# Lower bounds formed later, a first block scaled in halves, transposes on two PSUM tags and unread matmuls, in a stick-breaking and HGRN2 block on one core

## The chip, the core and the metric

The kernel runs on one core of one Trainium2 chip. A core has five engines, each working off its own instruction queue in order: TensorE (PE in the profile, with its weight loads as PEld), VectorE (DVE), ScalarE (ACT), GpSimd (POOL) and SyncE (SP, which here only issues transfers). Engines wait for each other through semaphores. The metric is the device time of one execution in microseconds (us); smaller is better.

## The reference

One residual block works on 16 learned meta rows followed by 1024 frames, each 1024 wide, all in float32:

```python
u = _rmsnorm(h, norm_g[l])
proj = u @ w_in[l]
(sb_q, sb_k, sb_v, sb_gate, hg_q, hg_f, hg_i, hg_gate,
 gate_sb, gate_hg) = jnp.split(proj, bounds, axis=-1)
y_sb = _stick_breaking(sb_q, sb_k, sb_v) * silu(sb_gate)
o_hg = _group_rmsnorm(_hgrn2(hg_q, hg_f, hg_i, lb_all[l]), hg_norm_g[l])
y_hg = o_hg * silu(hg_gate)
merged = (sigmoid(gate_sb) * (y_sb @ w_sb_out[l])
          + sigmoid(gate_hg) * (y_hg @ w_hg_out[l]))
h = h + merged @ w_out[l]
return _rmsnorm(h, final_norm_g)[:, N_META:N_META + S]
```

The lower bounds `lb_all` are a softmax over two rows of logits, one bound for each of 512 key channels. They enter only the forget gate of the HGRN2 branch, `f = lb + (1 - lb) * sigmoid(f_logit)`.

## The kernel before

**Whole program.** A float32 factor is kept as a rounded high part and a low remainder, and a product is three TensorE matmuls (high by high, high by low, low by high). In time order the program has a start (norm, transposes), four first projection groups of 128 columns (`first_g`), the wide projections made with seven products for eight (`prep`, `product`, the matmuls of L410), the attention with further projections laid between, the recurrence, and the output projection. This case is about the first two.

**The start.** The 1040 rows are nine blocks b0 to b8 of 128 rows (b8 has 16). `norm_g` is spread over the partitions into `gbc` by two matmuls with a row of ones (L146) and two VectorE copies (L147). For each block, in this order in the code:

- `stats`: ScalarE squares the block and sums it (L172), GpSimd makes the inverse root (L173, L174) into an `s` tile.
- `scaled`: VectorE multiplies the block `xb` by that and by `gbc`, in place (L180); TensorE transposes it in two halves of four 128 x 128 pieces (L185), each half into a PSUM tile of tag `tr`, which has two buffers; ScalarE rounds each half into `uh` (L187).
- `low_part`: VectorE writes the remainder into `ul` (L195), and ScalarE copies the PSUM half back into `xb` as floats (L196). A `tr` buffer is free once L187, L195 and L196 have read it.

Weights arrive as `wr` and are split in four quarters by ScalarE (`wh`, L119) and VectorE (`wl`, L124), for the first group behind b0 and for the second behind b2; those of the third group (`w3`, L224 and L225) stand behind b3. At the end VectorE forms sums and differences of the blocks for the seven products (`further`, L205 to L213).

**The first groups.** Groups 0, 1 and 2 are taken together by quarters of the rows: 24 matmuls of each group on rows 0 to 255 (blocks b0 and b1), then of each on the next quarter, and so on (`first_q`); group 3 follows alone. An accumulator is one of three PSUM buffers of tag `acc`; ScalarE copies it out (L320), and the copy goes to DRAM from ScalarE's queue.

**What sets the order.** The code above is written once, and a scheduler of the tile framework places each engine's instructions by its own estimates; the engines then run their lists strictly in order. The lower bounds stand late in the code:

```python
V.tensor_tensor(lbd, lbl[:, 0], lbl[:, 1], op=ALU.subtract)
omlb = sb("omlb", [P, 4])
S.activation(lb, lbd, AF.Sigmoid)
S.activation(omlb, lbd, AF.Sigmoid, scale=-1.0)
```

They have no other input than a small transfer (L84), and the scheduler places them at the head of the lists of VectorE and ScalarE. Their first reader is the forget gate (L704), in the attention.

Of the kernel before, what the change touches and what calls it, by code (L numbers as in the profile page):

```python
# [11 lines left out]
AF = mybir.ActivationFunctionType  # L12
ALU = mybir.AluOpType
PSUM = bass.MemoryType.PSUM

P = 128
D = 1024
# [4 lines left out]
NB = SEQ // P  # L22
# [23 lines left out]
def block_kernel(ctx: ExitStack, tc: tile.TileContext, x, meta, norm_g, w_in, w_sb_out,  # L46
                 w_hg_out, w_out, hg_norm_g, hg_lb_logits, final_norm_g, out):
    nc = tc.nc
    V, S, G, T = nc.vector, nc.scalar, nc.gpsimd, nc.tensor
# [5 lines left out]
    def nm(s):  # L55
        uid[0] += 1
        return f"{s}_{uid[0]}"
# [7 lines left out]
    def sb(tag, shape, dt=F32):  # L65
        p = base if tag in HOME else here[-1]
        return p.tile(shape, dt, tag=tag, name=nm(tag), bufs=BUFS.get(tag, 1))

    def ps(tag):
        return psum.tile([P, 512], F32, tag=tag, name=nm(tag), bufs=PB[tag])  # L70

    def kept(name, shape, dt=F32):
        return dram.tile(shape, dt, tag=name, name=nm(name))
# [4 lines left out]
    ident = sb("ident", [P, P])  # L78
    make_identity(nc, ident)
    mhalf = sb("mhalf", [P, 8])  # L80
    G.memset(mhalf, -0.5)

    lbl = sb("lbl", [P, 2, 4])
    nc.gpsimd.dma_start(lbl, hg_lb_logits.rearrange("r (h p) -> p r h", p=P))  # L84
# [12 lines left out]
    def fetch_w(src, col, chunks):  # L97
        if chunks > NC // 2:
            raw = sb("wr", [P, NC, P])
        else:  # L100
            if not half_rows:
                t = sb("wl", [P, 2, NC // 2, P])
                half_rows.extend((t[:, 0], t[:, 1]))
            half_rows.reverse()
            raw = half_rows[0]
        nc.sync.dma_start(raw[:, :chunks], src[:, col:col + P].rearrange("(c p) n -> p c n", p=P))
        return raw
# [20 lines left out]
    uh = sb("uh", [P, NC, L], F32R)  # L128
    ul = sb("ul", [P, NC, L], F32R)
    ones = sb("sg", [1, P])  # L130
# [7 lines left out]
    start = ExitStack()  # L138
    here.append(start.enter_context(phase("start")))

    gbc = sb("gbc", [P, D])
    row = sb("w3", [1, D])
    nc.scalar.dma_start(row, norm_g)
    for hf in range(2):
        acc = ps("acc")
        T.matmul(acc, ones, row[:, hf * 512:(hf + 1) * 512], start=True, stop=True)  # L146
        V.tensor_copy(gbc[:, hf * 512:(hf + 1) * 512], acc)  # L147

    FIRST = [C_HI + P * h for h in range(4)] 
    w3 = sb("w3", [P, 2, NC, P], F32R)  # L150
    xbs, raws = [], []
    for b in range(NB + 1):
# [9 lines left out]
        if b in (1, 3):  # L162
            raws.append(fetch_w(w_in[0], FIRST[b // 2], NC))
    w_first = []

    blk = [dict(rows=P if b < NB else NM, t0=P * b) for b in range(NB + 1)]
# [10 lines left out]
    def scaled(b):  # L177
        v = blk[b]
        rows, xs = v["rows"], xbs[b]
        V.scalar_tensor_tensor(xs[:rows], xs[:rows], v["r"][:rows, 0:1], gbc[:rows], op0=ALU.mult, op1=ALU.mult)  # L180
        v["tp"] = []
        for c4 in range(2):
            tp = ps("tr").rearrange("p (c n) -> p c n", c=4)
            for c in range(4):
                T.transpose(tp[:, c, :rows], xs[:rows, (c4 * 4 + c) * P:(c4 * 4 + c + 1) * P], ident[:rows, :rows])  # L185
            v["tp"].append(tp[:, :, :rows])
            S.activation(uh[:, c4 * 4:c4 * 4 + 4, v["t0"]:v["t0"] + rows], v["tp"][c4], AF.Copy)  # L187

    def low_part(b):

# [24 lines left out]
    for b in range(NB + 1):  # L215
        stats(b)
        scaled(b)
        low_part(b)
        if b in (0, 2):
            w_first.append(load_w(None, None, NC, raws[b // 2], eng=V))  # L220
        if b == 3:
            raw = fetch_w(w_in[0], FIRST[2], NC)
            for c in range(0, NC, SH):
                S.activation(w3[:, 0, c:c + SH], raw[:, c:c + SH], AF.Copy)  # L224
                V.tensor_tensor(w3[:, 1, c:c + SH], raw[:, c:c + SH], w3[:, 0, c:c + SH].bitcast(F32), op=ALU.subtract)  # L225
            w_first.append((w3[:, 0], w3[:, 1]))
# [13 lines left out]
    def proj(col, pieces, evac, begin=None, after=()):  # L240
        return group(w_in[0], col, NC, pieces, u_operand, evac, begin, after)
# [75 lines left out]
    def keep_raw(to):  # L317
        def ev(acc, t0, n):
            c = sb("sg", [P, 512])
            S.activation(c[:, :n], acc, AF.Copy)  # L320
            nc.scalar.dma_start(to[:, t0:t0 + n], c[:, :n])
        return ev

    kept_i = [kept(f"hi{h}", [P, L]) for h in range(4)]
    kept_f = [kept(f"hf{h}", [P, L]) for h in range(len(FIRST) - 4)]
    first_g = [proj(FIRST[h], QUART if h < 3 else FULL, keep_raw((kept_i + kept_f)[h])) for h in range(len(FIRST))]
    for g, w in zip(first_g, w_first):
# [333 lines left out]

    lb = sb("lb", [P, 4])
    lbd = sb("lbd", [P, 4])
    V.tensor_tensor(lbd, lbl[:, 0], lbl[:, 1], op=ALU.subtract)
    omlb = sb("omlb", [P, 4])
    S.activation(lb, lbd, AF.Sigmoid)
    S.activation(omlb, lbd, AF.Sigmoid, scale=-1.0)

    masks, anchor = {}, []

# [576 lines left out]
```

## Time and profile before

| | |
|---|---|
| median of 3 runs | 941.91 us (940.26 to 943.6) |
| profiled execution | 941.53 us |
| its span in the trace | 939.7 us |
| TensorE busy | 900.0 us, 96% of the span |
| VectorE, ScalarE, GpSimd busy | 675.0, 390.6, 248.7 us |

The span is the time between the first and the last recorded instruction; 1.83 us of the execution lie around it. Rows of the timeline give the start in us, the busy time in us, the engine, the line, the operation, what it writes and reads with shapes, the count, and in brackets how long the engine stood idle before it and what ended that. Where several instructions are merged into a row, the busy time is of all of them. The lines on which the prediction rests are quoted there.

### The profile page before, as it was taken

What the parts mean: (1) busy time and instruction counts of PE and PEld (TensorE: products, weight loads), DVE (VectorE), ACT (ScalarE), POOL (GpSimd) and SP (SyncE); (2) the same over time, 40 slices, a digit from 0 to 9 for tenths busy, and PEclk for the clock granted to TensorE, in tenths of its full rate; (3) what the DMA queues carried; (4) which work ended last, traced back from release to release, by engine and by line L of the source; (5) the groups of instructions that cost most, each with busy time, mean ns of one, the idle gap of its engine ahead of it and who ended that gap; (6) DMA issues with size and microseconds to landing.
All of it is one profiled execution on the core that took longest, in us unless ns stands there. A gap on an engine that the chain in (4) does not pass through costs nothing. (4 is left out here: it accounts for less than half of the span.)

```text
span 939.7 us, 13713 instructions
## 1 busy us (share of the span) xinstructions
PE 900.0 (96%) x5000; PEld 781.4 (83%) x5000; DVE 675.0 (72%) x1242; ACT 390.6 (42%) x892; POOL 248.7 (26%) x263
## 2 busy tenths in 40 slices
PE   5999999999999999999999999998989899999996
PEld 4898888888889998898898888897968688888885
DVE  5893446555433477888887898868697788897886
ACT  6824333343333455555565565132314145323341
POOL 3026445544442211132111111121212000003552
PEclk9999999999999999999999999999999999999999
DMA  8123543333336122221132222121111338564212
GB/s 271 52 63 100 160 145 112 101 118 118 113 113 184 63 80 78 68 68 57 57 113 64 72 80 79 57 79 57 56 56 45 102 101 284 186 213 163 107 45 91
DMA packets 89078, 98.04 MB, mean 104 GB/s; under 512 B 4513, under 2 KB 63777, under 8 KB 89010
## 3 DMA queue, kind: packets, MB, share of 16 engines
q1 hardware_dynamic: 75120, 73.51, 25.6%
q10 hardware_dynamic: 13826, 23.64, 6.9%
q8 instruction: 40, 0.66, 0.3%
q14 instruction: 28, 0.23, 0.1%
q0 software_dynamic: 64, 0.01, 0.1%
HBM read 71.94 MB, written 25.20 MB: 103 GB/s over the span
## 5 line engine op out<-in xcount | busy, mean ns | idle before, releaser
L264 PE MATMUL acc<-uh,wh 128*128 128x346 f32 (+4 forms) x536 | 192.3, 359 | 0.0
L264 PE MATMUL acc<-ul,wh 128*128 128x346 f32 (+4 forms) x536 | 184.9, 345 | 0.4 <-DVE ul L195 0.4
L264 PE MATMUL acc<-uh,wl 128*128 128x346 f32 (+4 forms) x536 | 183.9, 343 | 0.0
L124 POOL TENSOR_TENSOR wl<-wr,wh 128x256 fp32r<-128x256 f32 x92 | 80.4, 897 | 361.1 <-ACT wh L119 345.6
L264 PEld LDWEIGHTS acc<-uh,wl 128*128 128x128 f32 x536 | 101.5, 189 | 6.6
L264 PEld LDWEIGHTS acc<-uh,wh 128*128 128x128 f32 x536 | 101.7, 190 | 3.9 <-ACT uh L187 0.2
L264 PEld LDWEIGHTS acc<-ul,wh 128*128 128x128 f32 x536 | 101.9, 190 | 3.4 <-DVE ul L195 0.7
L399 POOL TENSOR_TENSOR pw<-su,pw 128x512 fp32r<-128x512 f32 x44 | 58.5, 1349 | 51.2 <-ACT pw L398 51.2
L572 ACT ACTIVATE ab<-z 128x456 f32<-128x456 f32 (+6 forms) x112 | 50.0, 448 | 30.7 <-PE z L570 30.4
L575 DVE TENSOR_TENSOR_SCAN ab<-ab,later 128x456 f32<-128x456 f32 (+3 forms) x64 | 55.2, 863 | 6.0 <-ACT ab L572 5.4
L615 DVE TENSOR_TENSOR wt<-tr,wt 128x512 fp32r<-128x512 f32 (+1 forms) x80 | 50.3, 630 | 12.6 <-ACT wt L614 11.0
L399 POOL TENSOR_TENSOR pw<-wr,pw 128x512 fp32r<-128x512 f32 x33 | 43.6, 1321 | 54.7 <-ACT pw L398 54.6
L410 PE MATMUL acc<-th,pw 128*128 128x512 f32 x176 | 57.8, 389 | 0.0
L626 PE MATMUL av<-wt,v 128*128 128x256 f32 x320 | 54.1, 287 | 3.6 <-DVE wt L615 2.0
L570 PE MATMUL z<-stk,q 128*128 128x456 f32 (+6 forms) x224 | 56.6, 333 | 0.0
L614 ACT ACTIVATE wt<-tr 128x512 fp32r<-128x512 f32 (+1 forms) x80 | 44.2, 555 | 29.3 <-PE tr L612 29.0
L119 ACT ACTIVATE wh<-wr 128x256 fp32r<-128x256 f32 x100 | 36.3, 410 | 47.5 <-PE acc L264 25.0
L398 ACT ACTIVATE pw<-su 128x512 fp32r<-128x512 f32 x44 | 26.2, 627 | 68.9 <-DVE su L393 47.8
L626 PEld LDWEIGHTS av<-wt,v 128*128 128x128 f32 x320 | 46.8, 188 | 8.6 <-DVE wt L615 4.0
L789 DVE COPY_PREDICATED ab<-mask,z 128x192 f32<-128x192 uint8 (+2 forms) x144 | 45.3, 350 | 11.0 <-PE z L780 9.7
L579 DVE TENSOR_TENSOR_SCAN ab<-ab 128x348 f32<-128x348 f32 (+4 forms) x48 | 46.9, 976 | 6.9 <-ACT ab L572 5.5
L780 PE MATMUL z<-wt,stk 128*128 128x192 f32 x192 | 37.8, 332 | 10.9 <-DVE wt L771 9.8
(335 smaller groups left out, 2057.1 us busy)
## 6 DMA issues: line engine op xcount, KB each, us to landing
wr<-in_w_in SPq DMA_DIRECT2D x48, 512.0 KB, 4.2
q<-q SPq DMA_DIRECT2D x32, 256.0 KB, 4.1
wr<-in_w_out SPq DMA_DIRECT2D x16, 512.0 KB, 4.2
sg<-gate SPq DMA_DIRECT2D x24, 256.0 KB, 3.6
gate<-sg ACTq DMA_DIRECT2D x20, 256.0 KB, 2.0
xb<-in_x SPq DMA_DIRECT2D x7, 512.0 KB, 8.5
gate<-co ACTq DMA_DIRECT2D x12, 256.0 KB, 2.6
pt<-hi SPq DMA_DIRECT2D x4, 520.0 KB, 3.2
```

Source lines behind the costliest of these rows:

```text
L124: eng.tensor_tensor(lo[:, cs], raw[:, cs], h[:, cs].bitcast(F32), op=ALU.subtract)
L264: T.matmul(acc, a, b, start=(k == 0), stop=(k == total - 1))
L399: G.tensor_tensor(t[:, 1], d[key], t[:, 0].bitcast(F32), op=ALU.subtract)
L410: T.matmul(acc, t[:, part // 2, c], (bh, bl, bh)[part][:, c], start=(c == part == 0), stop=(c == 3 and part == 2))
L570: T.matmul(z, qt[:, k, qo + qi * P:qo + (qi + 1) * P], st["k"][hh][:, c0:c1], start=(k == 0), stop=(k == 1))
L572: S.activation(a[:, c0:c1], z, AF.Sigmoid, scale=-1.0)
L575: ins = V.tensor_tensor_scan(w, w, later[:, WS - (n - c0):][:, ::-1], 1.0, op0=ALU.mult, op1=ALU.max)
L579: V.tensor_tensor_scan(w, w, w, a[:, c1:c1 + 1], op0=ALU.mult, op1=ALU.bypass)
L614: S.activation(wt[:, 0, lo:], tp[:, lo:], AF.Copy)
L615: V.tensor_tensor(wt[:, 1, lo:], tp[:, lo:], wt[:, 0, lo:].bitcast(F32), op=ALU.subtract)
L626: T.matmul(self.av, st["v"][hh][:, 2 * gg + j], wt[:, part, where[j]:where[j] + 256], start=(gg == g and part == 0 and j == 0), stop=False)
L789: V.copy_predicated(dst[:, :, :, d * h:], mask[:, :, :, :n * h].to_broadcast([P, 2, m, n * h]), z[:, :, k, :, lo * h:(lo + n) * h])
```

## The change

Four edits, all in the start:

```diff
     G.memset(mhalf, -0.5)
+    S.activation(sb("s4", [P, 8]), mhalf, AF.Square)
...
     for hf in range(2):
         acc = ps("acc")
-        T.matmul(acc, ones, row[:, hf * 512:(hf + 1) * 512], start=True, stop=True)
+        spread = T.matmul(acc, ones, row[:, hf * 512:(hf + 1) * 512], start=True, stop=True)
         V.tensor_copy(gbc[:, hf * 512:(hf + 1) * 512], acc)
 
+    def keep_busy(n, after):
+
+        with tc.issue_after(after.ins):
+            idle = ps("av")
+            for _ in range(n):
+                T.matmul(idle[:, :P], ident, ident, start=True, stop=True)
+
+    keep_busy(10, spread)
...
-        V.scalar_tensor_tensor(xs[:rows], xs[:rows], v["r"][:rows, 0:1], gbc[:rows], op0=ALU.mult, op1=ALU.mult)
+        for cs in ((slice(0, 512), slice(512, D)) if b == 0 else (slice(0, D),)):
+            v["scaled"] = V.scalar_tensor_tensor(xs[:rows, cs], xs[:rows, cs], v["r"][:rows, 0:1], gbc[:rows, cs],
+                                                 op0=ALU.mult, op1=ALU.mult)
         v["tp"] = []
         for c4 in range(2):
-            tp = ps("tr").rearrange("p (c n) -> p c n", c=4)
+            tp = ps(("tr", "z")[b % 2]).rearrange("p (c n) -> p c n", c=4)
             for c in range(4):
-                T.transpose(tp[:, c, :rows], xs[:rows, (c4 * 4 + c) * P:(c4 * 4 + c + 1) * P], ident[:rows, :rows])
+                last = T.transpose(tp[:, c, :rows], xs[:rows, (c4 * 4 + c) * P:(c4 * 4 + c + 1) * P], ident[:rows, :rows])
             v["tp"].append(tp[:, :, :rows])
-            S.activation(uh[:, c4 * 4:c4 * 4 + 4, v["t0"]:v["t0"] + rows], v["tp"][c4], AF.Copy)
+            v["last"] = S.activation(uh[:, c4 * 4:c4 * 4 + 4, v["t0"]:v["t0"] + rows], v["tp"][c4], AF.Copy)
+        if b == 0:
+            keep_busy(8, last)
...
-    V.tensor_tensor(lbd, lbl[:, 0], lbl[:, 1], op=ALU.subtract)
     omlb = sb("omlb", [P, 4])
-    S.activation(lb, lbd, AF.Sigmoid)
-    S.activation(omlb, lbd, AF.Sigmoid, scale=-1.0)
+    with tc.issue_after(blk[NB]["scaled"].ins):
+        V.tensor_tensor(lbd, lbl[:, 0], lbl[:, 1], op=ALU.subtract)
+    with tc.issue_after(blk[NB]["last"].ins):
+        S.activation(lb, lbd, AF.Sigmoid)
+        S.activation(omlb, lbd, AF.Sigmoid, scale=-1.0)
```

The lower bounds are placed behind the last block's scaling and rounding; a Square on eight columns at the head of ScalarE's list loads its table there. Block b0 is scaled in two halves. Odd blocks are transposed into tag `z` (two buffers, not used otherwise this early), even ones into `tr`. Ten matmuls of the identity by itself follow the two that spread `norm_g`, and eight more the transposes of b0; nothing reads what they write. The scheduler then lays out the lists of TensorE, VectorE and ScalarE anew over the start and the first groups; behind the first few weight parts of the seven products each engine's list is as before, and those of GpSimd and SyncE are the same throughout.

TensorE, from the beginning of its list, before (`xb_102`, `xb_105` are blocks b0 and b1, `acc_427` and `acc_455` the accumulators of groups 0 and 1 on the first quarter):

```order
L146 MATMUL acc_95<-w_17_93,sg_76 128x512
L146 MATMUL acc_98<-w_17_93,sg_76 128x512
L185 MATMUL tr_132<-ident_63,xb_102 128x128 x4
L185 MATMUL tr_138<-ident_63,xb_102 128x128 x4
L185 MATMUL tr_165<-ident_63,xb_105 128x128 x4
L185 MATMUL tr_171<-ident_63,xb_105 128x128 x4
L264 MATMUL acc_427<-uh_74,wh_148 128x256
L264 MATMUL acc_455<-uh_74,wh_204 128x256
```

The same place now (`xb_115`, `xb_118`, `xb_122` are b0, b1 and b2; L155 is the unread matmul, L196 the transpose, L277 the projection's matmul):

```order
L147 MATMUL acc_97<-w_18_95,sg_78 128x512
L147 MATMUL acc_100<-w_18_95,sg_78 128x512
L155 MATMUL av_103<-ident_63 128x128 x10
L196 MATMUL tr_146<-ident_63,xb_115 128x128 x4
L196 MATMUL tr_152<-ident_63,xb_115 128x128 x4
L155 MATMUL av_158<-ident_63 128x128 x8
L196 MATMUL z_188<-ident_63,xb_118 128x128 x4
L196 MATMUL z_194<-ident_63,xb_118 128x128 x4
L196 MATMUL tr_211<-ident_63,xb_122 128x128 x4
L196 MATMUL tr_217<-ident_63,xb_122 128x128 x4
L277 MATMUL acc_450<-uh_76,wh_171 128x256
```

The unread matmuls stand in front of the transposes of b0 and of b1, and b2, whose transposes lay among the first group's matmuls, now comes ahead of all of them.

TensorE at the seam between the first and the second quarter of the rows, before (`acc_483` is group 2 on the first quarter, `acc_511` group 0 on the second; `xb_115` and `xb_117` are here b4 and b5):

```order
L185 MATMUL tr_260<-ident_63,xb_115 128x128 x4
L264 MATMUL acc_483<-uh_74,w_20_101 128x256 x2
L264 MATMUL acc_483<-ul_75,w_20_101 128x256
L264 MATMUL acc_483<-uh_74,w_20_101 128x256 x2
L264 MATMUL acc_483<-ul_75,w_20_101 128x256
L264 MATMUL acc_483<-uh_74,w_20_101 128x256
L185 MATMUL tr_277<-ident_63,xb_117 128x128 x4
L264 MATMUL acc_511<-uh_74,wh_148 128x256
L264 MATMUL acc_511<-ul_75,wh_148 128x256
```

The same seam now (`acc_506` is group 2 on the first quarter, `acc_534` group 0 on the second; `xb_130`, `xb_132`, `xb_134`, `xb_136` are b5 to b8):

```order
L196 MATMUL z_306<-ident_63,xb_130 128x128 x4
L277 MATMUL acc_506<-ul_77,w_22_114 128x256
L277 MATMUL acc_506<-uh_76,w_22_114 128x256 x2
L277 MATMUL acc_506<-ul_77,w_22_114 128x256
L277 MATMUL acc_506<-uh_76,w_22_114 128x256
L196 MATMUL tr_323<-ident_63,xb_132 128x128 x4
L196 MATMUL tr_329<-ident_63,xb_132 128x128 x4
L196 MATMUL z_346<-ident_63,xb_134 128x128 x4
L196 MATMUL z_352<-ident_63,xb_134 128x128 x4
L196 MATMUL tr_369<-ident_63,xb_136 128x16 x4
L196 MATMUL tr_375<-ident_63,xb_136 128x16 x4
L277 MATMUL acc_534<-uh_76,wh_171 128x256
```

The transposes of b5's second half to b8, which were spread through the second and third quarters, all stand ahead of the second quarter's first matmul, and those of b6 to b8 follow each other with nothing between.

ScalarE at that time, now (L198 rounds into `uh`, L209 copies back into `xb`, L181 squares, L333 copies an accumulator out):

```order
L209 ACTIVATE xb_130<-z_300 128x512
L181 ACTIVATE sg_364,s_80_362<-xb_136 16x1024
L209 ACTIVATE xb_130<-z_306 128x512
L209 ACTIVATE xb_132<-tr_323 128x512
L209 ACTIVATE xb_132<-tr_329 128x512
L198 ACTIVATE uh_76<-z_346 128x4x128
L198 ACTIVATE uh_76<-z_352 128x4x128
L198 ACTIVATE uh_76<-tr_369 128x4x16
L198 ACTIVATE uh_76<-tr_375 128x4x16
L333 ACTIVATE sg_475<-acc_450 128x256
```

Before, the first copy of an accumulator (L320) stood ahead of the rounding of b5; now it stands behind that of b8, and the second half of b5 is copied back only behind the square of b8.

## The prediction

> **What bounds it now.** I read busy time by stage first, cut where the waits end.
>
> ```profile
> 0.00:17.10 17.10, 7.45 (x20) 4.30 (x20) 8.45 (x14) 10.12 (x21) 6.87 (x17) 1.00 0.91 291
> 17.10:33.60 16.50, 14.27 (x101) 13.50 (x100) 13.50 (x21) 15.20 (x34) 3.71 (x10) 1.00 0.42 117
> 33.60:74.90 41.30, 41.30 (x320) 40.59 (x318) 36.31 (x74) 17.84 (x41) 10.06 (x9) 1.00 0.18 57
> 74.90:300.00 225.10, 225.10 (x1008) 186.48 (x1006) 104.77 (x156) 79.12 (x141) 103.23 (x86) 1.00 0.40 125
> ```
>
> Columns: length, then PE, PEld, DVE, ACT, POOL busy. From 33.6 to 300 us TensorE is never idle, so whatever the start gains or loses there goes to the end. Between 17.1 and 33.6, though, ScalarE is busy 15.20 of 16.50 us, more than TensorE (14.27). In that stage ScalarE's list, not TensorE, is nearly full. TensorE's waits up to 140 us:
>
> ```profile
> PE tr L185 <- DVE xb L180: 4.9, 1, 4.9
> PE tr L185 <- ACT xb L196: 3.7, 2, 2.3
> ```
>
> The change aims at these and at the clock. Next the timeline of ScalarE and VectorE:
>
> ```profile
> 7.21 0.16 DVE L664 TENSOR_TENSOR lbd<-lbl 128x4 f32<-128x4 f32 x1 [6.17 <-DMA lbl<-in_hg_lb_logits]
> 9.30 1.33 ACT L119 ACTIVATE wh<-wr 128x256 fp32r<-128x256 f32 x4 [0.55 <-DMA wr<-in_w_in]
> 10.54 1.04 ACT L172 ACTIVATE sg<-xb 128x1024 bf16<-128x1024 f32 x1
> 11.58 1.04 ACT L172 ACTIVATE sg<-xb 128x1024 bf16<-128x1024 f32 x1
> 12.62 1.06 ACT L187 ACTIVATE uh<-tr 128x512 fp32r<-128x512 f32 x2
> 13.58 1.05 ACT L172 ACTIVATE sg<-xb 128x1024 bf16<-128x1024 f32 x1
> 14.72 1.20 ACT L196 ACTIVATE xb<-tr 128x512 f32<-128x512 f32 x2
> 15.81 0.41 ACT L119 ACTIVATE wh<-wr 128x256 fp32r<-128x256 f32 x1
> 15.20 2.47 DVE L180 SCALAR_TENSOR_TENSOR xb<-xb,s,gbc 128x1024 f32<-128x1024 f32 x2
> 17.59 1.28 DVE L195 TENSOR_TENSOR ul<-tr,uh 128x512 fp32r<-128x512 f32 x2
> ```
>
> From 9.30 ScalarE is back to back to 15.81, and its start at 9.30 is set by the first weight tile's transfer, not by the lower bounds.
>
> **Lower bounds and halves: nothing.** The wait to 7.21 goes, so b0 can be squared, scaled and transposed up to some 2 us earlier, and the halves let its first transposes go 0.6 us sooner. But ScalarE's list still has the four weight quarters next, at 9.30, then two squares, and reads b0's transposes at 12.62 as before. b1's square stays at 10.54, hence its scaling too. Worth nothing unless that transfer lands earlier, which nothing here moves. The new place costs a second table load and two short Sigmoids, behind a VectorE row near the end of `further`:
>
> ```profile
> L666 ACT ACT_TABLE_LOAD x1 | 1.3, 1283 | 1.4 <-PEq L1236 1.4
> 68.00 0.23 DVE L213 TENSOR_TENSOR tl<-xb,th 128x64 fp32r<-128x64 f32 x1
> 63.72 0.40 ACT L320 ACTIVATE sg<-acc 128x272 f32<-128x272 f32 x1 [2.63 <-PE acc L264]
> 71.16 0.32 PE L264 MATMUL acc<-uh,wh 128*128 128x346 f32 x1
> ```
>
> ScalarE will stand at `lb` until about 68, and behind it waits the copy that now runs at 63.72; its buffer is wanted by the third piece of group 3 at about 71.2. Free by about 68.9, it is 2.3 us early: nothing, and the price if VectorE ended 3 us later would be 0.7 us.
>
> **Unread matmuls.** What they are for is seen here:
>
> ```profile
> 2.42 3.75 PE L146 MATMUL acc<-w,sg 1*128 1x512 f32 x4 [2.42 <-DMA w<-in_norm_g]
> 11.06 1.97 PE L185 MATMUL tr<-ident,xb 128*128 128x128 f32 x8 [4.89 <-DVE xb L180]
> 18.33 0.58 PE L264 MATMUL acc<-ul,wh 128*128 128x256 f32 x1 [0.36 <-DVE ul L195]
> 21.70 0.41 PE L264 MATMUL acc<-uh,wh 128*128 128x256 f32 x1
> 21.91 0.33 PE L264 MATMUL acc<-ul,wh 128*128 128x256 f32 x1
> 45.94 0.28 PE L264 MATMUL acc<-uh,wh 128*128 128x256 f32 x1
> 51.65 0.28 PE L264 MATMUL acc<-uh,w 128*128 128x256 f32 x1
> ```
>
> Up to 21.9 these matmuls follow each other at 0.21 us; from 45.94 to 51.65 stand 48 of them, 0.119 each. TensorE works at half pace until 3.6 us into its first unbroken stretch. At full pace the work from 18.33 to 21.9 would take 1.6 us less. The unread ones cost: two recorded passes each (two L146 matmuls are four), each pass as long as a transpose of as many columns, eight of which take 1.97 with the last one's tail: 0.21 slow, so 0.43 for a matmul and half that fast. Ten from 6.2 end by 10.4 at worst, b0's eight transposes by 12.3, and ScalarE reads their first half at 12.62. Eight more end by 15.5 if slow throughout, 1.4 us after b1 is scaled; by 14.0 if fast by then. Bounds of this edit: nothing to 1.4 us later. I take nothing, since TensorE is then unbroken from 2.4 on, far longer than 3.6 us.
>
> The Trainium skill ("TensorE: Matmul & The Clock Gate", Part 1) says that the clock halves by default and opens after one busy window of about 3.4 us, free-running, and closes after an idle one; the 3.6 us here agrees. Its Part 4 says transposes do not count as busy. By that rule the gate could close again between the last unread matmul and the first real one, which is the slow rival below.
>
> **Two tags, and the new order: the main term.** b1 and b3 no longer wait for a `tr` buffer, and b2 goes ahead of the matmuls. But b5's second half to b8 must now be through before the second quarter's first matmul, so I follow ScalarE's new list. Durations:
>
> ```profile
> 20.21 0.20 ACT L172 ACTIVATION_READ_ACCUMULATOR sg<-xb 128x1 f32 x1
> 21.36 1.28 DVE L180 SCALAR_TENSOR_TENSOR xb<-xb,s,gbc 128x1024 f32<-128x1024 f32 x1 [1.15 <-POOL s L174]
> 22.19 0.60 PE L185 MATMUL tr<-ident,xb 128*128 128x128 f32 x4
> 22.83 0.60 ACT L187 ACTIVATE uh<-tr 128x512 fp32r<-128x512 f32 x1 [0.33 <-PE tr L185]
> 29.66 0.59 ACT L196 ACTIVATE xb<-tr 128x512 f32<-128x512 f32 x1
> 30.14 0.60 ACT L187 ACTIVATE uh<-tr 128x512 fp32r<-128x512 f32 x1
> ```
>
> Start to start ScalarE takes 1.04 for a square, 0.31 for a weight quarter, 0.48 for a rounding or copy; VectorE 1.20 for a scaling, 0.60 for a remainder. From a square's end to its scaling, over GpSimd, 0.95 (20.41 to 21.36). Transposes to rounding 0.64.
>
> ScalarE rounds b1 from 15.7. Then come a weight quarter, b2's rounding, three more quarters with the copies of b1 and b2 between, b3's rounding: eight half-blocks and four quarters with a little waiting, 6.2 us. It squares b4 at 21.9, copies b3 back and takes four quarters, squares b5 from 25.2 to 26.3. b4's scaling on VectorE is thus 24.0 to 25.3, and TensorE, done with groups 0 and 1 at 24.5, waits 0.9 for it. b5's scaling is 27.3 to 28.6. Behind it VectorE has b4's remainders, b6's scaling (ends 31.0, TensorE has waited 1.0), b7's (ends 32.2) and only then b5's remainders, 32.1 to 33.4. These free the `z` buffers for b7: ScalarE copies the first half back at 32.8 to 33.4, then stands on the square of b8, and the second half at 34.3 to 34.9. So TensorE waits 1.6 and then 1.1 us between b7's halves. b8's scaling follows its square (ends 34.4) at 35.4 to 36.7, its transposes at 36.7, waiting 1.3; ScalarE rounds them at 37.3 and 37.6, and only then copies out group 0's first accumulator, at 37.8. The second quarter needs that buffer: its first matmul comes at **38.2**.
>
> Against that, what before makes of the same work:
>
> ```profile
> 33.69 0.36 PE L264 MATMUL acc<-uh,wh 128*128 128x256 f32 x1
> 63.52 0.32 PE L264 MATMUL acc<-uh,wh 128*128 128x348 f32 x1
> 74.97 0.40 PE L410 MATMUL acc<-uh,pw 128*128 128x512 f32 x1
> ```
>
> It begins the second quarter at 33.69 with five half-blocks and b8 still to transpose, and reaches the seven products at 74.97. Without them the quarter is 72 matmuls of 0.119, 8.57 us, and from 45.94 to 74.97 there are none: 29.03. Together 37.6 us, so the change is even if the quarter begins at 37.4. It begins at 38.2: **0.8 us later**. VectorE, idle 5 of the 41.3 us to 74.9, still ends `further` in time for the seven products. The clock gain is no term of its own: it shortens TensorE's waits inside this stretch.
>
> Bounds: GpSimd's small operations are held while VectorE scales,
>
> ```profile
> 12.80 1.28 DVE L180 SCALAR_TENSOR_TENSOR xb<-xb,s,gbc 128x1024 f32<-128x1024 f32 x1 [0.46 <-POOL s L174]
> 12.85 1.28 POOL L173 TENSOR_SCALAR s<-s 128x1 f32<-128x1 f32 x1
> ```
>
> and b7's would start within 0.1 us of b6's scaling: 0.7 us more if it comes second. The other way, errors of 0.1 us at some ten hand-overs make 1 us. So 0.2 us earlier to 1.5 later.
>
> Sum: 939.7 span + 1.83 around it + 0.8 = 942.4. The run that was profiled, 941.53, lies 0.4 under the median of 941.91.
>
> **Rivals.** *TensorE-bound (faster).* If TensorE alone set the pace, it would gain the 1.6 of the clock, the 1.4 us that is left of the 3.7 for `tr` buffers beside the 2.3 before b1, and about 1.0 for b2's transposes, which leave the dense part: 4.0 us, 937.5. For it: 96% busy. Against it: ScalarE's 15.20 of 16.50, and the accumulator copy behind b8. It takes ScalarE reaching that copy by about 33 instead of 37.8.
>
> *The clock falls back (slower).* From about 12 to 17.2 TensorE would hold only transposes.
>
> ```profile
> 746.51 1.54 PE L780 MATMUL z<-wt,stk 128*128 128x192 f32 x8 [2.25 <-DVE wt L771]
> 748.82 1.46 PE L780 MATMUL z<-wt,stk 128*128 128x192 f32 x8
> ```
>
> An idle 2.25 us did not slow it there, but 5 us is not shown. Then b2's transposes end 0.8 us late, and ScalarE's whole chain with them: 39.05. If half pace lasts past the stalls to 25, the first quarter's matmuls become late themselves: 40.1. With GpSimd's hold 943.2 to 944.9. It decides from a gate still shut when groups 0 and 1 should end, 24.5.
>
> *The unread matmuls do not speed TensorE at all.* Then b1 is the 1.4 us late, and ScalarE's chain behind it: 39.6, 943.7.
>
> **Chances.** The forecast 0.62, TensorE-bound 0.12, clock falling back 0.16, no speed-up 0.10. What a measurement here can tell from no change is 0.3%, 2.8 us. The forecast and the slow cases lie mostly inside it; of these 0.14 lies beyond with the spread of the runs, of TensorE-bound nearly all: faster 0.12, same 0.74, slower 0.14. The range takes the forecast's bounds (941.3 to 943.1), the slow cases to 944.9, and 1 us for the spread of medians below: 940.0 to 945.0.
>
> **What would show it.** Right: the matmul of 256 columns at 0.12 us from its first row; ScalarE still at 9.30 on the weights and dense to about 31; TensorE waiting four or five times between 24 and 38, longest on b7 and b8; the second quarter near 38.2, the seven products near 75.8. Wrong: the second quarter before 36, or ScalarE idle for more than 2 us between 16 and 34, or a new wait of TensorE at 68 to 76.

## The result and the profile after

The changed kernel takes **946.26 us** (median of 8 runs, 944.38 to 947.51) against 942.75 for the kernel before (8 runs beside it, 940.26 to 943.74): a ratio of 1.0041, 95% interval 1.0026 to 1.0055. It is slower by some 3.9 us, by more than the 0.3% that was to be told from no change, and lies above the range. The profiled execution took 945.4 us, its span 943.7.

Stages of the changed kernel, cut where its waits end (columns as before: PE, PEld, DVE, ACT, POOL busy, granted clock, transfers):

```profile
17.10:31.90 14.80, 13.80 (x102) 12.95 (x101) 12.60 (x21) 14.22 (x32) 3.17 (x8) 0.89 0.48 132
31.90:39.60 7.70, 3.38 (x24) 2.60 (x24) 7.00 (x11) 6.10 (x15) 1.16 (x2) 0.85 0.00 1
39.60:44.10 4.50, 4.50 (x21) 4.50 (x22) 4.50 (x13) 1.82 (x6) 0.00 (x0) 0.50 0.28 89
44.10:79.24 35.14, 35.14 (x269) 35.14 (x269) 25.75 (x54) 10.97 (x25) 11.16 (x11) 1.00 0.20 62
79.24:300.00 220.76, 220.76 (x980) 182.17 (x979) 104.75 (x155) 77.77 (x136) 100.39 (x81) 1.00 0.38 122
```

As forecast, ScalarE's list is nearly full until 31.9 (14.22 of 14.80). Then come 7.7 us in which TensorE works for 3.38. From 39.60 on it is never idle, but in the first 4.5 us of that the clock column reads 0.50 and it gets through 21 matmuls. Its waits and its timeline (start, busy time, line, what it writes and reads, count, idle time before):

```profile
PE tr L196 <- DVE xb L190: 3.9, 4, 1.6
PE z L196 <- ACT xb L209: 2.1, 2, 1.3
PE z L196 <- DVE xb L190: 0.9, 1, 0.9
PE acc L277 <- ACT sg L333: 0.6, 1, 0.6
```

```profile
10.36 1.04 PE L196 MATMUL tr<-ident,xb 128*128 128x128 f32 x8
11.23 1.95 PE L155 MATMUL av<-ident 128*128 128x128 f32 x16
14.10 1.09 PE L196 MATMUL z<-ident,xb 128*128 128x128 f32 x8 [0.92 <-DVE xb L190]
16.58 1.72 PE L196 MATMUL tr<-ident,xb 128*128 128x128 f32 x8 [1.39 <-DVE xb L190]
...
31.92 1.06 PE L196 MATMUL tr<-ident,xb 128*128 128x128 f32 x8 [0.73 <-DVE xb L190]
34.25 0.66 PE L196 MATMUL z<-ident,xb 128*128 128x128 f32 x4 [1.27 <-ACT xb L209]
35.76 0.66 PE L196 MATMUL z<-ident,xb 128*128 128x128 f32 x4 [0.85 <-ACT xb L209]
38.01 1.00 PE L196 MATMUL tr<-ident,xb 16*128 16x16 f32 x8 [1.60 <-DVE xb L190]
39.60 0.58 PE L277 MATMUL acc<-uh,wh 128*128 128x256 f32 x1 [0.59 <-ACT sg L333]
...
44.21 0.28 PE L277 MATMUL acc<-uh,wh 128*128 128x256 f32 x1
...
79.24 0.40 PE L423 MATMUL acc<-uh,pw 128*128 128x512 f32 x1
```

The unread matmuls did what they are for at first: b0's eight transposes take 1.04 where they took 1.97. But b2's, at 16.58, are slow again. In the run b6 to b8 TensorE waits before every pair or half, for the blocks that were named beforehand. The second quarter begins at 39.60 at half pace.

This accounts for the seven products: they begin at 79.24 instead of 74.97, 4.27 later. The quarter began at 39.60, where 37.37 would have been even (74.97 less the 29.03 and 8.57 us of the prediction): 2.23. And its first 4.5 us held 21 matmuls where 0.119 each makes 38: 17 matmuls, 2.02. Together 4.25.

### The profile page after: what moved, and what is told of

The parts are those of the page before. It is cut to its first block, busy times and chain, and to the rows that moved or that the text cites. A ratio compares the mean times of both kernels' runs of the same rounds, so it can differ in the third digit from the quotient of the medians.

```text
span 943.7 us, 13785 instructions
## 1 busy us (share of the span) xinstructions
PE 906.7 (96%) x5036; PEld 789.2 (84%) x5036; DVE 676.1 (72%) x1243; ACT 390.6 (41%) x894; POOL 249.3 (26%) x263
## 5 line engine op out<-in xcount | busy, mean ns | idle before, releaser
L277 PE MATMUL acc<-uh,wh 128*128 128x346 f32 (+4 forms) x536 | 193.4, 361 | 0.6 <-ACT sg L333 0.6
L277 PE MATMUL acc<-ul,wh 128*128 128x346 f32 (+4 forms) x536 | 185.3, 346 | 0.1
L277 PE MATMUL acc<-uh,wl 128*128 128x346 f32 (+4 forms) x536 | 184.6, 344 | 0.0
L277 PEld LDWEIGHTS acc<-uh,wl 128*128 128x128 f32 x536 | 102.5, 191 | 6.5
L277 PEld LDWEIGHTS acc<-uh,wh 128*128 128x128 f32 x536 | 102.9, 192 | 4.4 <-ACT sg L333 0.7
L277 PEld LDWEIGHTS acc<-ul,wh 128*128 128x128 f32 x536 | 103.0, 192 | 3.1 <-DVE ul L208 0.4
```

What stands on the lines that cost most here:

```text
L277: T.matmul(acc, a, b, start=(k == 0), stop=(k == total - 1))
```

## The experiments

Each time was taken over five rounds beside the kernel before on the same chip; a ratio is to that, with its 95% interval. Each of these kernels computes all that the reference asks for. The last two columns are of the one profiled execution: when ScalarE begins on the first weights, which is when their transfer lands, and when the seven products begin. The landing differs by up to 1.4 us between executions and moves what follows; in the profile of before it is at 9.30, and the products are at 74.97.

| | ratio to before | first weights | seven products |
|---|---|---|---|
| the change | 1.0041 [1.0026, 1.0055] | 9.42 | 79.24 |
| e4, two tags alone | 1.0053 [1.0040, 1.0067] | 9.66 | 79.16 |
| e3, the change with one tag | 0.9986 [0.9976, 0.9995] | 9.53 | 76.12 |
| e7, unread matmuls alone | 0.9985 [0.9976, 0.9995] | 10.25 | 75.53 |
| e9, lower bounds alone | 1.0000 [0.9988, 1.0012] | 9.83 | 76.46 |
| e10, halves alone | 1.0013 [1.0003, 1.0023] | 9.59 | 75.55 |
| e8, the change without unread matmuls | 1.0019 [1.0011, 1.0028] | 9.70 | 79.20 |
| e5, second tag for b1 alone | 0.9995 [0.9984, 1.0006] | 9.73 | 76.14 |
| e1, the change, run of b5 to b8 filled | 1.0011 [1.0000, 1.0022] | 10.72 | 78.44 |
| e2, the same, b1 filled too | 1.0008 [0.9999, 1.0016] | 9.66 | 78.46 |
| e12, as e1, filled with transposes | 1.0006 [0.9993, 1.0020] | 10.09 | 79.31 |
| e6, as e5, b1 filled | 0.9983 [0.9974, 0.9992] | 9.67 | 75.76 |
| e11, as e3, b1 filled | 0.9982 [0.9971, 0.9992] | 9.75 | 76.23 |
| e13, as e6, filled with transposes | 0.9982 [0.9970, 0.9993] | 9.41 | 75.28 |

### Which part: e4, e3, e7, e9, e10

e4 is the kernel before with this line of the change alone:

```diff
-            tp = ps("tr").rearrange("p (c n) -> p c n", c=4)
+            tp = ps(("tr", "z")[b % 2]).rearrange("p (c n) -> p c n", c=4)
```

> The kernel of before with nothing but the two tags. Its list of TensorE has the same run of transposes, b5's to b8's, ahead of the second quarter. Theory: the quarter begins late (39 to 40.5) and slow, products at 78.5 to 80.5, ratio about 1.004. Rival (the tags only show their cost together with the unread matmuls or with the moved lower bounds): products before 76, ratio under 1.0015.

Measured: 948.09 us, ratio 1.0053, a little over what its theory gave; the quarter begins at 40.18 at half pace, as it says. The profiled execution, 944.58, was the fastest of six, and the median is 3.5 us above it, so its 79.16 understates the loss. e3 is the change without that line.

> The changed kernel with all transposes on the one tag; lower bounds, halves and unread matmuls stay. Its list of TensorE has the transposes of b5 to b8 spread through the second and third quarters again. Theory (the two tags, through the order that the scheduler makes of them, are what costs): no stretch without matmuls after 20 us, the clock stays open, the products begin between 72 and 75.2; ratio 0.997 to 1.000. Rival (the unread matmuls or the later lower bounds cost): products later than 76.5, ratio over 1.0015.

Measured: 941.6 us, ratio 0.9986, within its theory. The products came at 76.12, later than the 75.2 it allows, and the clock did not stay open: it reads 0.50 from 18.68 to 22.09. The two tags are the whole loss, and more; the rest of the change gains a little. e7 is the kernel before with the two calls of `keep_busy` alone.

> The kernel before with the 18 unread matmuls alone (one tag, the blocks unhalved, the lower bounds where they were); all lists beside the unread matmuls are those of before. Theory 1 (ScalarE's list sets the second quarter's start; the unread matmuls only bring TensorE's full pace forward): the first stretch's matmuls run at 0.12 us for part of 15 to 22, the products stand at 74 to 76, median 941.5 to 943.5, ratio 0.998 to 1.001. Rival (TensorE's half pace until 21.9 was a cost of its own): 939 to 941, ratio under 0.9975. Rival 2 (unread matmuls cost by themselves): 945 or more.

Measured: 940.42 us, ratio 0.9985, at the faster edge of theory 1 and short of its rival. Its matmuls run at full pace where before's ran at half, yet its products are no earlier than before's 74.97; its first weights came 0.95 us later:

```profile
19.34 0.39 PE L274 MATMUL acc<-ul,wh 128*128 128x256 f32 x1 [1.05 <-DVE ul L205]
19.56 0.28 PE L274 MATMUL acc<-uh,wl 128*128 128x256 f32 x1
...
75.53 0.40 PE L420 MATMUL acc<-uh,pw 128*128 128x512 f32 x1
```

e9 shows why one execution cannot settle that. It is the kernel before with the last hunk of the change (and the Square) alone, with the blocks in before's order on TensorE.

> The kernel before with the lower bounds alone moved behind the normalised blocks, and the small Square at the program's beginning (one tag, whole blocks, no unread matmuls); TensorE's and VectorE's orders of the blocks are those of before. Theory 1: nothing, since ScalarE's start hangs on the first weight tile at 9.3 and the second table load is covered: 941.5 to 943, ratio 0.9990 to 1.0010, products at 74.5 to 75.5. Rival (the second table load, some 1.3 us on ScalarE near 65 to 68, is on the path): 1 to 1.5 us slower, ratio 1.0010 to 1.0016. Rival 2 (ScalarE's earlier start helps): ratio under 0.9990.

Measured: 942.65 us, ratio 1.0000: the lower bounds cost nothing. But its products came at 76.46, 1.49 after before's. Its matmuls of 256 columns are slow until 24.3, where before's pace changes at 21.9:

```profile
23.01 0.41 PE L265 MATMUL acc<-uh,wl 128*128 128x256 f32 x1
...
24.29 0.31 PE L265 MATMUL acc<-ul,wh 128*128 128x256 f32 x1
24.44 0.28 PE L265 MATMUL acc<-uh,wl 128*128 128x256 f32 x1
...
76.46 0.40 PE L411 MATMUL acc<-uh,pw 128*128 128x512 f32 x1
```

So 74.97 was an early one: with the same order the first weights came 0.53 us later in another execution, and TensorE's pace changed 2.4 us later. e10 is the kernel before with b0 scaled in halves alone.

> The kernel before with the first block's scaling in halves alone (one tag, no unread matmuls, the bounds where they were). Its TensorE list differs from before's: b2's two halves are transposed together, 13 matmuls stand before them and 35 behind. Theory 1: b0's first transposes come 0.6 earlier and save nothing, because ScalarE's list is full: 941.5 to 943.5, ratio 0.9985 to 1.0010. Rival (the scheduler's new order by itself costs, as with two tags): 944 or more.

Measured: 943.33 us, ratio 1.0013. The median is inside theory 1, the ratio a little above it: the halves, which the scheduler answers with another order of TensorE (b2's two halves together), cost some 1.2 us. The single execution's 75.55 does not show where; that stays open.

### The order: e5 and e8

e5 leaves the second tag to b1 alone:

```diff
-            tp = ps(("tr", "z")[b % 2]).rearrange("p (c n) -> p c n", c=4)
+            tp = ps(("tr", "z")[b % 2 if b < 2 else 0]).rearrange("p (c n) -> p c n", c=4)
```

> The changed kernel with the second tag for the block b1 alone; b2 to b8 transpose into tr again. TensorE's list then has 14 to 28 matmuls between each pair of transposes of b3 to b7 instead of the run b5 to b8 with none; the unread matmuls, the halves and the lower bounds stay. Theory 1 (the run of transposes costs: TensorE waits in it and its clock gate closes behind it): the second quarter begins at 37.5 to 39 at 0.12 us a matmul from its first row, the seven products at 75 to 77, and the median is 941 to 943.5, ratio 0.997 to 1.001. Rival (what costs is the second tag as such, by the first two blocks' transposes that come before any matmul): median 945.5 to 947.5, ratio 1.003 to 1.005, as with both tags throughout. Rival 2 (unread matmuls alone cost, by whatever they hold up): 945 or more here too.

Measured: 941.72 us, ratio 0.9995, as theory 1 has it: what costs is the order that the scheduler makes of b5 to b8 with two tags, not the second tag for the first blocks. (No run has both tags throughout in the order of before, so tag and order are not parted further.) One step of that theory fell, though: the quarter began earlier than I had said, at 34.17, and at half pace all the same:

```profile
34.17 0.58 PE L277 MATMUL acc<-uh,wh 128*128 128x256 f32 x1 [1.59 <-ACT sg L333]
```

```profile
33.60:37.02 3.42, 2.85 (x13) 2.86 (x14) 2.98 (x6) 1.68 (x5) 0.88 (x2) 0.50 0.24 79
```

e8 is the change without its two calls of `keep_busy`.

> The changed kernel without the 18 unread matmuls (two tags, halves and lower bounds stay). Its list differs from the changed kernel's: there are 12 to 24 matmuls behind each pair of b2 to b5, and only b6 and b7's pair stand together. Theory 1: TensorE runs at half pace at first as before, but no second closing, second quarter at 38 to 39.5 at 0.12 us a matmul, median 942 to 944.5, ratio 0.999 to 1.002. Rival (the two tags as such): 945.5 to 948.5, ratio 1.003 or more, as with the tags alone (948.1).

Measured: 944.17 us, ratio 1.0019, at the slow edge of theory 1; "no second closing" was wrong. Here TensorE waits 4.1 us before b6's transposes, the clock column reads 0.50 from 36.06 to 42.89, and the quarter begins inside that:

```profile
35.02 1.06 PE L195 MATMUL tr<-ident,xb 128*128 128x128 f32 x8 [4.11 <-DVE xb L189]
...
38.62 0.56 PE L274 MATMUL acc<-uh,wh 128*128 128x256 f32 x1
38.98 0.41 PE L274 MATMUL acc<-ul,wh 128*128 128x256 f32 x1
```

Taking the unread matmuls out of the change thus makes it faster (1.0019 against 1.0041, the intervals just touch), though alone they gain (e7): without them the scheduler leaves only b6 and b7 together.

### The clock behind the run: e1 and e2

e1 is the change with four unread matmuls behind b5, b6 and each half of b7; the lists of ScalarE and VectorE stay as they are.

```diff
             v["tp"].append(tp[:, :, :rows])
+            if b in (5, 6, 7) and c4 == 1 or b == 7:
+                keep_busy(4, last)
```

> The changed kernel with sixteen more unread matmuls, four each behind the transposes of b5 and b6 and behind each half of b7, where TensorE waited 0.7 to 1.6 us at a time; the lists of ScalarE and VectorE are the same. Theory (the clock closes while TensorE holds only transposes and waits): the second quarter still begins near 39.6 us, its matmuls are 0.12 us apart from the first row, and the seven products begin near 77.2 instead of 79.24, so 2.0 us under the changed kernel and 2.2 over before (ratio about 1.0023). Rival (the slow matmuls from 39.6 to 44 have another cause than idleness, such as the traffic of the accumulator copies): they stay 0.21 us apart up to 44 and the products begin near 79.2, ratio about 1.0043.

Measured: 943.61 us, ratio 1.0011 where the change has 1.0041: 0.30% (0.18 either way, from the two intervals), 2.8 us, come back from work that nobody reads. In its profile the quarter begins even later, at 40.78, because the first weights came at 10.72, 1.30 us later than in the change, and made b1 late; TensorE, waiting 2.6 us for b1, then had a first closing of two windows (16.16 to 22.99). But the quarter is at full pace from the first row:

```profile
10.72 1.34 ACT L120 ACTIVATE wh<-wr 128x256 fp32r<-128x256 f32 x4 [4.19 <-DMA wr<-in_w_in]
...
40.78 0.39 PE L279 MATMUL acc<-uh,wh 128*128 128x256 f32 x1 [0.59 <-ACT sg L335]
41.00 0.28 PE L279 MATMUL acc<-ul,wh 128*128 128x256 f32 x1
...
78.44 0.40 PE L425 MATMUL acc<-uh,pw 128*128 128x512 f32 x1
```

From the quarter to the products are 37.66 us; in the change 39.64. That is the 2.0 us of the half pace. The record also has the mean granted clock of each whole execution, in which one window of 3.41 us at half pace is 0.0018: 0.987 to 0.990 in all eight of the change, 0.992 to 0.997 in the twelve of e1. So the clock was closed for longer in every execution of the change than in any of e1, not in the profiled ones alone. e2 adds four behind b1 (`b in (1, 5, 6, 7)`).

> As the last, and four more unread matmuls behind the transposes of b1. Theory (the first closing, before b2's transposes at 16.58, put ScalarE's chain 0.8 us late): b2's transposes take 0.4 a half instead of 0.85, the second quarter begins near 38.8 and the products near 76.4; ratio about 1.0015. Rival (the lateness over the forecast's 38.2 comes from GpSimd held behind VectorE at 15.2 us and the hand-overs alone): b2 is faster but the quarter stays at 39.4 to 39.6, products at 77.0 to 77.2.

Measured: 943.88 us, ratio 1.0008, no different from e1. In its profile the first closing is gone and b2's transposes take 1.06, but the quarter begins at 39.28, between the 38.8 of the theory and the 39.4 of its rival: b2's slow transposes explain little of the lateness. The second closing is there, from 39.34:

```profile
35.93:39.34 3.41, 2.11 (x21) 1.85 (x20) 2.71 (x4) 2.56 (x8) 0.58 (x2) 1.00 0.02 7
39.34:42.75 3.41, 3.41 (x16) 3.41 (x17) 3.41 (x10) 1.76 (x6) 0.00 (x0) 0.50 0.34 115
```

Whether a closing happens thus differs between executions. In cuts of 0.25 us the clock column puts its edges in the change at 16.82, 20.24, 37.30 and 44.13; in e5 at 16.54, 19.95, 33.60 and 37.02; in e12 at 17.29, 20.70, 41.18 and 44.59. Within an execution all lie a multiple of 3.41 us apart (17.06 is five, 20.48 six). So time is cut into windows of 3.41 us, set anew in each execution, and each closing takes one or two whole ones. Cut so, the change reads:

```profile
13.41:16.82 3.41, 1.34 (x10) 1.13 (x11) 3.02 (x4) 3.41 (x8) 3.04 (x4) 1.00 1.02 408
...
30.47:33.89 3.42, 1.78 (x15) 1.37 (x13) 3.42 (x5) 3.03 (x7) 0.53 (x1) 1.00 0.03 9
33.89:37.30 3.41, 1.31 (x8) 0.84 (x8) 2.71 (x5) 3.41 (x8) 1.16 (x2) 1.00 0.01 2
37.30:40.71 3.41, 2.11 (x13) 2.03 (x14) 3.41 (x9) 2.05 (x7) 0.00 (x0) 0.50 0.08 26
40.71:44.13 3.42, 3.42 (x18) 3.42 (x18) 3.42 (x8) 0.86 (x4) 0.00 (x0) 0.50 0.29 92
```

Behind the two windows in which TensorE was busy for 1.34 and 1.31 of 3.41 us the clock halves in the next; 1.78 left it open. It opened again behind a full window, not behind one with 2.11. The run of b6 to b8, 7.7 us long with 3.38 busy, is longer than two windows, so one whole window lies in it wherever they are set.

### Transposes or idle time: e12 and e13

The run holds transposes and waits. Is it closed over because transposes don't count, or because TensorE waits? e12 is e1 with eight unread transposes in place of each four unread matmuls, which take as long:

```diff
             for _ in range(n):
-                T.matmul(idle[:, :P], ident, ident, start=True, stop=True)
+                T.transpose(idle[:, :P], ident, ident)
+                T.transpose(idle[:, :P], ident, ident)
```

(There for the calls in the run alone.)

> The kernel of e1 with each group of four unread matmuls in the run of b5 to b8 replaced by eight unread transposes of the identity, which take TensorE as long (eight transposes 1.04, four matmuls in eight passes 1.06); the 18 earlier unread matmuls stay, ScalarE's and VectorE's lists the same. TensorE is as busy through the run as in e1. Theory 1a (the gate counts matmuls alone and closes over transposes, busy or not): the second quarter's first 15 to 25 matmuls run at 0.21 us, seven products 1.5 to 2 us later than the quarter's start would give at full pace, median 945 to 947.5, ratio 1.0030 to 1.0050, as without fill. Theory 1b (the gate counts TensorE's idle time): matmuls at 0.12 from the quarter's first row, median as e1, 943 to 944.5, ratio 1.0000 to 1.0022.

Measured: 943.84 us, ratio 1.0006, as e1: theory 1b. Its interval ends at 1.0020, below the 1.0030 of theory 1a, and the mean clock of its twelve executions, 0.992 to 0.996, is e1's and not the change's. Its windows, and below them those of e4:

```profile
34.36:37.77 3.41, 3.01 (x26) 2.56 (x25) 2.71 (x6) 3.41 (x8) 1.16 (x2) 1.00 0.01 2
37.77:41.18 3.41, 2.10 (x21) 1.79 (x20) 3.41 (x7) 2.42 (x8) 0.00 (x0) 1.00 0.08 26
41.18:44.59 3.41, 3.41 (x19) 3.41 (x18) 3.41 (x10) 0.92 (x4) 0.00 (x0) 0.50 0.28 94
```

```profile
32.92:36.34 3.42, 1.65 (x12) 1.18 (x12) 3.42 (x6) 3.03 (x7) 0.09 (x1) 1.00 0.00 0
36.34:39.75 3.41, 1.29 (x12) 0.99 (x12) 2.71 (x4) 2.56 (x7) 1.08 (x2) 1.00 0.01 2
39.75:43.16 3.41, 2.98 (x14) 2.98 (x15) 3.41 (x10) 2.25 (x8) 0.00 (x0) 0.50 0.27 90
```

In e12 a window with nothing but transposes on TensorE (34.36 to 37.77, busy 3.01) left the clock open, and a later one, with b8's wait and the wait for the accumulator in it, closed it: in this one execution the quarter was slow from 41.18 on all the same, because of where the window fell. In e4 two windows of transposes alone follow each other; 1.65 us busy left the clock open, 1.29 closed it. So transposes keep the clock open as matmuls do, and TensorE's idle time closes it.

e13 puts the same question at the first closing: e6 with eight transposes for its four matmuls behind b1.

> The kernel of e6 with the four unread matmuls behind b1 replaced by eight unread transposes, equally long; the rest the same. Theory 1a (transposes do not count): b2's transposes and the first matmuls behind them at half pace for about 3 us from 16.9, as in e5, median 0.5 to 1.2 us over e6, ratio 0.9990 to 1.0000. Theory 1b (idle time counts): b2's transposes in 1.06 us and the first matmuls at 0.12, median as e6, ratio 0.9975 to 0.9988.

Measured: 941.82 us, ratio 0.9982, b2's transposes in 1.06 us and no closing at all, as 1b has it. The interval (0.9970 to 0.9993) reaches into 1a's range, so it is e12 that carries the point.

### Better versions: e6 and e11

e6 is e5 with four more unread matmuls behind b1, e11 is e3 with the same:

```diff
-        if b == 0:
-            keep_busy(8, last)
+        if b < 2:
+            keep_busy(8 - 4 * b, last)
```

> The kernel of e5 with four unread matmuls more behind the transposes of b1 (ScalarE's and VectorE's lists the same). Theory 1, with the first closing (17 to 20 or so) as a cost of its own that ScalarE's full list hides in part: that closing is gone in most executions, median 0 to 1 us under e5, 940.5 to 943. Rival (ScalarE's list sets the stretch whatever TensorE's pace): equal to e5 within 0.5 us. Rival 2 (unread matmuls hold TensorE up): 0.5 us or more over e5.

> The kernel of e3 (the change with one tag) with four unread matmuls more behind the transposes of b1. Theory 1 (the first closing at some 18.8 to 22 costs a little, as between e5 and e6): 0 to 1 us under e3's 941.6, ratio 0.9975 to 0.9987. Rival (nothing to gain, ScalarE's list sets the stretch): ratio 0.9983 to 0.9992, no difference from e3. Rival 2 (they hold TensorE up): over 0.9992.

Measured: 940.76 us, ratio 0.9983, and 940.69, ratio 0.9982. Against e5 the fill is worth 0.12%, within theory 1, though the intervals overlap; b2's transposes, 1.94 in e5, show what it does:

```profile
16.89 1.94 PE L196 MATMUL tr<-ident,xb 128*128 128x128 f32 x8 [1.39 <-DVE xb L190]
```

```profile
16.82 1.06 PE L196 MATMUL tr<-ident,xb 128*128 128x128 f32 x8 [0.50 <-DVE xb L190]
```

e11 cannot be told from e3, and in its profile the first closing is there all the same (16.95 to 20.36). Both, like e7 and e13, are faster than the kernel before and than the change; they cannot be told from each other.

## Why the prediction was wrong, step by step

**What bounds the start.** Right. From 39.60 TensorE is never idle, and the 4.27 us at the products come out as 4.0 at the end of the span.

**Lower bounds: nothing.** Right (e9). **Halves: nothing.** Off by about 1.2 us (e10); the prediction followed b0 and not what the scheduler does to b2.

**Unread matmuls: nothing to 1.4 later, taken as nothing.** Alone they gain 1.4 us (e7, 0.9985; 0.5 to 2.3 by its interval), near the 1.6 that the TensorE-bound rival gave the clock; through which wait is not shown. "TensorE is then unbroken from 2.4 on" held only to 13.2, the end of the second batch; TensorE was busy for 1.34 us of the next whole window (13.41 to 16.82) and the clock closed from 16.82 to 20.24.

**Two tags: 0.8 later, the main term.** The place and the kind were right, the size was not: alone they cost 0.53%, 5.0 us (e4). TensorE waited where it was said to, before b4, b6, both halves of b7 and b8: 0.2, 0.7, 1.3, 0.9 and 1.6 against 0.9, 1.0, 1.6, 1.1 and 1.3. Two things failed in the sum.

First, the **missing term**: "The clock gain is no term of its own: it shortens TensorE's waits inside this stretch." The listed waits from b6 on come to 5.0 us between 30 and the quarter at 38.2, and were priced as lateness only. That such waits close the clock was not asked, although the gate had been weighed for the stretch from 12 to 17. It closed from 37.30 to 44.13 and cost 2.0 us of dense work, which nothing hides. It also slowed b8's own transposes: from these to the quarter are 1.59 us, but 1.23 in e2, where they ran at full pace:

```profile
38.05 0.64 PE L196 MATMUL tr<-ident,xb 16*128 16x16 f32 x8 [0.71 <-DVE xb L190]
```

Filling the run gave 2.8 us back in the medians (e1), and 2.0 between quarter and products in the profile.

Second, the **lateness**: 2.2 over the even point instead of 0.8. ScalarE, VectorE and GpSimd of the changed kernel show where the 1.4 between arise:

```profile
17.48 0.60 ACT L198 ACTIVATE uh<-tr 128x512 fp32r<-128x512 f32 x1 [0.33 <-PE tr L196]
18.33 0.60 ACT L198 ACTIVATE uh<-tr 128x512 fp32r<-128x512 f32 x1 [0.26 <-PE tr L196]
...
22.61 1.11 ACT L181 ACTIVATE sg<-xb 128x1024 bf16<-128x1024 f32 x1
```

```profile
35.28 0.61 DVE L218 TENSOR_TENSOR xb<-xb,xb 128x448 f32<-128x448 f32 x1
36.59 1.27 DVE L190 SCALAR_TENSOR_TENSOR xb<-xb,s,gbc 16x1024 f32<-16x1024 f32 x1 [0.70 <-POOL s L183]
```

```profile
35.32 0.62 POOL L182 TENSOR_SCALAR s<-s 16x1 f32<-16x1 f32 x1 [4.31 <-ACT sg L181]
```

ScalarE waits 0.6 us for b2's slow transposes and squares b4 at 22.61, forecast 21.9. Not much of these 0.7 goes back to the slow transposes, though: in e2, where they are quick, b4's square comes 12.99 us after the first weights, 13.19 in the change, since ScalarE then waits for VectorE instead. So they are worth 0.2; 0.1 more is the later landing of the first weights, and the rest is not told apart here. For b8 GpSimd's small operation takes 0.62 beside VectorE's, some 0.4 more than the 0.19 it takes alone, and the scaling comes at 36.59, forecast 35.4. The other 0.3 is spread over hand-overs.

**The rivals.** "The clock falls back" had the quarter at 39.05 to 40.1, and it came at 39.60. The closing that it named did come, and b2's transposes were slow, but by e2 that is 0.2 of the lateness: the place of the quarter fits by luck more than by its mechanism. It ended 2 us too low for want of the second closing. That TensorE sets the pace fell with ScalarE's full list, and that the unread matmuls do not speed TensorE with b0's 1.04.

**The rule that was weighed.** The Trainium skill ("TensorE: Matmul & The Clock Gate", Part 1) has the free-running window of about 3.4 us; the edges here, 3.41 us and its multiples apart, agree. Its Part 4 says of a transpose that "it doesn't count as PE-busy the same way"; e12 and the windows of e4 speak against that for the transposes here, and the closing that it led to came from idle time. Whether these transposes use the mode that the page means, the profile does not show.

**The comparison point.** The even point was taken from one execution of before, an early one: e9, with the blocks in the same order, had its products 1.49 us later. The landing of the first weights, from 9.30 to 10.72 in these profiles, is a part of that which no edit here moves. The median of before, 941.91 over the three executions on record then, is 942.75 over eight. All accounts from single profiles here carry an uncertainty of this size, and the medians decide.

## What to carry to other kernels

Price TensorE's waits twice: once for what they delay, and once for the clock. Where TensorE is busy for less than about half of a stretch of two windows (6.8 us; here 3.38 of 7.7), expect the dense work behind it to run at half pace for a window or more, by estimate up to 1.7 us for each, half of 3.41, that no other engine hides. A few unread matmuls in waits that end later than they do prevent much of it (e1), but look at the scheduler's order again once they are in: e8 lost less without them. More buffers can make a scheduler bunch short work that it had spread: read the new order for stretches in which the bounding engine only waits.

## What the hardware showed that was not expected

- The clock column shows the 0.50 of a closing, but not the half pace at the beginning of a program: before's row for 17.10 to 33.60 reads 1.00, though its matmuls follow each other at 0.21 us until 21.9. At the beginning the pace of matmuls of one shape is the surer sign.
- How busy a window must be is not pinned down: with TensorE busy 1.65 (e4) and 1.78 us (the change) the clock stayed open, with 1.71 (e3), 1.82 (e5), 2.10 (e12) and 2.11 (e2) it closed. In the last two the eight small transposes of b8 stand at 0.64 us of that, though they have 16 columns each; for the first two no reason is shown.
- GpSimd's one-column operations take longer beside VectorE. The bounds of the prediction show it for the first of the two, and it holds for the second too: the power of b3's sums, 0.55 us otherwise, took 1.64 while VectorE scaled b2:

```profile
14.18 0.55 POOL L183 TENSOR_TENSOR s<-s,mhalf 128x1 f32<-128x1 f32 x1
15.20 1.64 POOL L183 TENSOR_TENSOR s<-s,mhalf 128x1 f32<-128x1 f32 x1
```
